# Rewriting the hand-written order of the first stage of a hybrid encoder layer

## The chip, the cores and the metric

The kernel runs on one core of one Trainium2 chip. The metric is the device time of one execution in microseconds; the time of a kernel is the median of its runs. The time before is 1359.33 us (three runs, 1357.09 to 1360.18). One further execution was recorded by the hardware profiler; all views below are of that one.

## The reference

One layer over 4096 tokens of width 1024. An input projection, a windowed attention and a pooling group side by side, gates on both, and an output projection:

```python
h = rmsnorm(x, pre_norm_g)
q, k, v, g_a, u_p, g_p = split(h @ w_in)      # 512,128,128,512,512,512 columns
a = banded_attention(q, k, v, rel_bias, attn_sink) * silu(g_a)   # |i-j| <= 128, 8 heads of 64
p = multiscale_pool(u_p, pool_w, pool_scale) * silu(g_p)         # windows 2, 4, 8, 16, minus the token
mixed = concat([a, p]) @ w_out
out = x + rmsnorm(mixed, post_norm_g)
```

## The kernel before

**Numbers.** Every float32 operand of a large product is split into a float16 high part and a float16 low part; a product is the sum of three float16 products (high by high, low by high, high by low). Weights are scaled by a power of two that comes from their column norms (`sc`, its inverse `isc`), tokens by the inverse root of their row norms.

**Two stages.** The first stage (all of it inside one list, `plan`) computes g_p, g_a and u_p for all tokens and keeps them in DRAM (`ga_scr`, `yp_scr`). The second stage (a second list) computes q, k, v, the attention and the output projection, and is not rewritten by this change except for one operand of `gate`.

**Macro tiles.** The first stage takes 512 tokens at a time: macro tile 0 to macro tile 7. Macro tile 0 is plain: twelve weight tiles of 128 columns (0-3 g_p, 4-7 g_a, 8-11 u_p), four blocks each for tiles 0 and 2 (`mm_block`), one call of `mm` for each of the others. During it the weights are prepared: loaded to one of six `raw` slots, multiplied by the norm gain (`w_fold`, L343), squared (`w_square`, L370), summed over rows (`w_presum` on GpSimd L376, `w_norm` on TensorE L389), turned into the scale (`scale_pow`, five small VectorE steps), split (`w_high` L425, `w_low` L428); the u_p weights are multiplied by `pool_w` first (`u_prod` L355, `u_fold` L363). From pairs of tiles the sums of a Winograd form are built (`t_sums` L444, `t_high` L463, `t_low` L468). Macro tiles 1 to 7 use this form: seven products (`STEPS`) for each of three column groups QU (u_p), QP (g_p), QG (g_a), each product 24 matmuls (`product`, L902).

**Around a product.** After it comes `keep` (ScalarE, L914: the accumulator is copied out), `join` (VectorE, L928: it is added to a kept part) or a direct use (`direct_u`, `direct_gates`). A product that writes the same accumulator next waits for that. Gates are a Sigmoid on ScalarE (L939, L955) and a multiplication (`gate_mult`: GpSimd for QP, VectorE for QG, L946; `direct_mult`, L962). The pooling of the macro tile before (`pool_tile` on VectorE, L775 to L791; `pool_gate` on GpSimd, L799; `pool_store`) stands behind the joins of QU.

**The x of a macro tile.** Four natural blocks are loaded (`x_nat`, L251), squared with an accumulator on ScalarE (L191); the row norms are finished on GpSimd (`x_scale`, L200 and L203), written to DRAM (`rs_row`, L257) and read back spread over all partitions (`rb`, L259). Transposed x is loaded to `ybig` (`y_load`, L269), multiplied by `rb` (`y_scale`, L279), split into `xt` by a ScalarE copy and a VectorE subtraction (`x_hi` L285, `x_lo` L290), and summed in place (`x_sum`, L297).

**Order.** `due(t, fn, ...)` gives every step a planned time; the list is sorted by it, and each engine runs its steps strictly in that order. The planned times decide only the order: an engine whose next step is not ready waits, and all behind it wait with it. All DMAs of the kernel are issued by one queue, SP, in the same order.

Of the kernel before, what the change touches and what calls it, by code (L numbers as in the profile page):

```python
# [17 lines left out]
P = 128  # L18
S = 4096
D = 1024  # L20
# [42 lines left out]
U_EVAC = 2.0**-14  # L63
GP_EVAC = 2.0**-30
GA_EVAC = 2.0**-44
# [4 lines left out]
def hybrid_layer(ctx: ExitStack, tc, io, out):  # L70
# [18 lines left out]
    nc.vector.memset(ones16, 1.0)  # L89
    mhalf = const.tile([P, 1], F32, name="mhalf")  # L90
# [16 lines left out]
    cgs = const.tile([P, 8], F32, name="cgs")  # L107
# [17 lines left out]
    def scale_pow(dst, n2, floor, top):  # L125

        m2 = comm.tile([P, 1], F32, name="m2", tag="m2")
        nc.vector.tensor_reduce(out=m2, in_=n2, axis=mybir.AxisListType.X, op=ALU.max)
# [21 lines left out]
    with ExitStack() as actx:  # L150
# [8 lines left out]
        pw = pa1.tile([P, 4, P], F32, name="pw")  # L159

# [15 lines left out]
        def first_use():  # L176

            nc.scalar.activation(pa1.tile([P, 1], F32, name="dummya"), mhalf, AF.Sigmoid)
# [77 lines left out]
        def rs_row(m):  # L256
            nc.sync.dma_start(rs_scr[m].rearrange("(b p) -> p b", p=P), rs_t[m][:, 1])  # L257
            rb_t[m] = pa1.tile([P, T], F32, name=f"rb{m}", tag="rb")
            nc.sync.dma_start(  # L259
                rb_t[m], rs_scr[m].rearrange("(o t) -> o t", o=1).to_broadcast([P, T])  # L260
            )
# [80 lines left out]
        def w_fold(si, eng=nc.vector):  # L342
            eng.tensor_tensor(out=raw_k(si), in0=raw_k(si), in1=gb, op=ALU.mult)  # L343
# [4 lines left out]
        def u_prod(j, half):  # L348

            wt = raw_of(("u", j))  # L350
            pp = psa.tile([P, 4, P], F32, name=f"wup{j}_{half}", tag="wup", bufs=2)
# [16 lines left out]
        def w_square(si):  # L368
            sq_t[si] = pa.tile([P, KT, P], BF16, name=f"sq{si}", tag="sq")
            nc.scalar.activation(sq_t[si], raw_k(si), AF.Square)  # L370

        def w_presum(si, ns=(4, 2)):

            sq = sq_t[si]
            for n in ns:
                nc.gpsimd.tensor_tensor(  # L376
                    out=sq[:, :n], in0=sq[:, :n], in1=sq[:, n : 2 * n], op=ALU.add
                )

        def w_norm(si, n, by=None, of=None):  # L380

            sq = sq_t.pop(si)
            key = si if of is None else of
            first = key not in n2_t
            if first:
                n2_t[key] = psa.tile([P, 1 if of is None else 2, P], F32, name=f"n2_{key}", tag="n2")
            o = n2_t[key][:, 0 if first else 1]
            for k in range(n):
                nc.tensor.matmul(  # L389
                    o, ones16 if by is None else by[:, k, :], sq[:, k, :],  # L390
                    start=(k == 0 and first), stop=(k == n - 1), skip_group_check=True,
                )

        def w_scale(si):
            scale_pow(
                sc[:, si : si + 1], n2_t.pop(si).rearrange("p a c -> p (a c)"), 1e-20, W_SCALE
            )

        def pair_scale(s1):

            scale_pow(
                sc[:, s1 : s1 + 3 : 2], n2_t.pop(s1).rearrange("p a c -> p (a c)"), 1e-20, W_SCALE
            )
# [7 lines left out]
        def pair_gate(s1):  # L411
            for t, e in ((cg, 1.0), (cgs, 1.0 / (GA_EVAC if s1 >= A_GA else GP_EVAC))):
                nc.vector.tensor_scalar(
                    out=t[:, s1 : s1 + 3 : 2], in0=isc[:, s1 : s1 + 3 : 2], scalar1=e / H_SCALE,
                    scalar2=None, op0=ALU.mult,
                )

# [93 lines left out]
        def row_prod():  # L511
            row_t["p"] = psa.tile([NH, 512], F32, name="fp", tag="wup", bufs=2)
# [71 lines left out]
        def out_scales():  # L584
# [3 lines left out]
                out=rowsc[:, 0:4], in0=isc[:, A_GA : A_GA + 4],  # L588
# [17 lines left out]
        def out_square(k):  # L606
            w = raw_of(("o", k))
            nc.scalar.activation(w, w, AF.Square, scale=rowsc[:, k : k + 1])

        def out_sum(k):  # L610

            sq = raw_of(("o", k))
            if k == KT - 1:
                sq = out_t["s"] = pa.tile([P, D], BF16, name="wosq", tag="sq")
            nc.gpsimd.tensor_tensor(
                out=sq, in0=raw_of(("o", k)), in1=raw_of(("o", k - 1)), op=ALU.add
            )
            raw_put(("o", k - 1))
            if k == KT - 1:
                raw_put(("o", k))  # L620

        def out_norm():
            out_t["n"] = [psa.tile([P, 512], F32, name=f"no{i}", tag="n2") for i in range(2)]
            for i in range(2):
                nc.tensor.matmul(
                    out_t["n"][i], ones16, out_t["s"][:, i * 512 : (i + 1) * 512],
                    start=True, stop=True,
                )

        def out_sigma():  # L630
            nm = pa.tile([P, 2], F32, name="nmx", tag="nmx")
            for i in range(2):
                nc.vector.tensor_reduce(
                    out=nm[:, i : i + 1], in_=out_t["n"][i], axis=mybir.AxisListType.X, op=ALU.max
                )
            scale_pow(sigma, nm, 1e-36, W_SCALE)
# [7 lines left out]


# [86 lines left out]
        def sigmoid(si):  # L732
            nc.scalar.activation(
                plain_dest(si), acc_t[0, si], AF.Sigmoid, scale=cg[:, si : si + 1]
            )

        def silu(si, scale):

            s = plain_dest(si)
# [1293 lines left out]
```

## Time and profile before

| | |
|---|---|
| median of 3 runs | 1359.33 us |
| profiled execution | 1366.74 us, span 1365.0 us |
| mean granted TensorE clock | 0.949 |
| busy: TensorE, VectorE, ScalarE, GpSimd | 1198.0, 979.2, 706.4, 393.8 us |
| last matmul of the first stage ends | 656.5 us after the span's start |

The page of the profile gives busy time by engine; a timeline lists merged instructions with, in brackets, the idle time of that engine before them and what released it; the waits add these up; the groups by line give count, busy time and the mean of one.

### The profile page before, as it was taken

The numbers are of one execution on the slowest core, as the hardware profiler recorded it, in microseconds if no ns is written. First come the engines' busy times: TensorE is split into PE (matmuls) and PEld (weight loads), VectorE is DVE, ScalarE is ACT, GpSimd is POOL, SyncE is SP. The second block draws the span as 40 slices with busy tenths as digits, with TensorE's granted clock in tenths as the row PEclk, the third lists the DMA queues.
The fourth block names the chain that finished last, engine by engine and source line by source line (L and its number), as shares of the span: only waits on it lengthen the run. The fifth ranks groups of instructions, "written<-read, shape, count | busy, mean of one in ns | idle before, by whom it ended". The sixth has DMA issues, their size and how long they took to land. (4 is left out here: it accounts for less than half of the span.)

```text
span 1365.0 us, 25715 instructions
## 1 busy us (share of the span) xinstructions
PE 1198.0 (88%) x10186; PEld 867.8 (64%) x10186; DVE 979.2 (72%) x1800; ACT 706.4 (52%) x1524; POOL 393.8 (29%) x363
## 2 busy tenths in 40 slices
PE   5776859787795859689789999999999999999998
PEld 4532658677684748578666667666676666766654
DVE  5477857565837768584867787777877778777796
ACT  4263624344343626433266666756667566575663
POOL 1120212112243102011212443334433344333431
PEclk9788989989897979889999999999999999999999
DMA  8132735443455557456479577665776567765594
GB/s 226 63 128 72 248 108 198 136 168 111 142 178 175 192 164 248 145 168 184 153 206 254 128 190 202 170 149 154 185 208 170 146 159 182 200 170 139 146 257 122
DMA packets 304569, 230.09 MB, mean 169 GB/s; under 512 B 213776, under 2 KB 270736, under 8 KB 299456
## 3 DMA queue, kind: packets, MB, share of 16 engines
q1 hardware_dynamic: 304448, 228.45, 58.7%
q8 instruction: 79, 1.29, 0.4%
q14 instruction: 42, 0.34, 0.1%
HBM read 115.14 MB, written 62.44 MB: 130 GB/s over the span
## 5 line engine op out<-in xcount | busy, mean ns | idle before, releaser
L902 PEld LDWEIGHTS <-wa 128*128 128x128 f16 x3528 | 357.0, 101 | 123.5 <-issue 71.2
L902 PE MATMUL ch<-xt,wa 128*128 128x256 f16 x2016 | 224.3, 273 | 7.3 <-ACT cbig L914 5.1
L1305 PEld LDWEIGHTS <-raw 128*128 128x128 f16 x1920 | 186.8, 98 | 39.5 <-issue 9.6
L902 PE MATMUL cl<-xt,wa 128*128 128x256 f16 x1008 | 135.4, 304 | 56.7 <-ACT u L950 32.5
L1374 ACT ACTIVATE p<-p,nm 128x385 f32<-128x385 f32 (+1 forms) x256 | 153.0, 599 | 57.2 <-POOL p L1357 38.0
L1404 DVE SCALAR_TENSOR_TENSOR pn<-p,rd,pn 128x384 f16<-128x384 f32 (+1 forms) x256 | 156.6, 658 | 26.1 <-ACT pn L1396 25.4
L1305 PE MATMUL aq<-xt,raw 128*128 128x256 f16 x1536 | 173.1, 273 | 0.0
L1613 PE MATMUL ms<-wo,ys 128*128 128x512 f16 x720 | 162.7, 379 | 0.0
L1363 DVE CUSTOM_DVE_ANT_0 p<-s,ybig,nsink 128x384 f32<-128x384 f32 (+1 forms) x256 | 155.9, 665 | 1.4 <-PE s L1342 1.1
L1396 ACT ACTIVATE pn<-p,rd 128x384 f16<-128x384 f32 (+1 forms) x256 | 136.3, 597 | 23.5 <-ACT p L1374 21.6
L799 POOL TENSOR_TENSOR yt<-yt,gp 128x512 f32<-128x512 f32 x32 | 50.6, 1583 | 323.1 <-DVE yt L791 243.7
L1613 PEld LDWEIGHTS <-ys 128*128 128x128 f16 x720 | 69.1, 98 | 82.8 <-issue 4.2
L1613 PE MATMUL m<-wo,y 128*128 128x512 f16 x540 | 119.6, 379 | 0.6 <-POOL y L1519 0.4
L279 DVE TENSOR_TENSOR ybig<-ybig,rb 128x1024 f32<-128x1024 f32 x28 | 33.4, 1221 | 88.3 <-DMA rb<-rs_scr 83.9
L1613 PEld LDWEIGHTS <-y 128*128 128x128 f16 x540 | 51.5, 98 | 65.2 <-issue 4.4
L1649 POOL TENSOR_TENSOR mo<-mo,ybig 128x512 f32<-128x512 f32 x39 | 64.8, 1661 | 87.5 <-ACT jkb L1638 86.3
L285 ACT CAST xt<-ybig 128x1024 f16<-128x1024 f32 x56 | 57.9, 1036 | 61.0 <-DVE ybig L279 48.1
L290 DVE TENSOR_TENSOR xt<-ybig,xt 128x1024 f16<-128x1024 f32 x56 | 69.5, 1249 | 14.7 <-ACT xt L285 14.7
L1342 PE MATMUL s<-k_all,q 64*128 64x384 f16 (+2 forms) x912 | 73.8, 298 | 3.0 <-ACT q L1295 1.6
L848 PE MATMUL a<-xt,wa 128*128 128x512 f16 x240 | 59.3, 406 | 18.4 <-ACT wa L425 16.8
L1381 DVE TENSOR_SCALAR den<-den 128x4 f32<-128x4 f32 x64 | 17.4, 272 | 76.5 <-ACT p L1374 76.4
L1484 PE MATMUL o<-pt,vv 128*64 128x256 f16 x1128 | 68.1, 274 | 2.8 <-DMA pt<-pn 2.7
(178 smaller groups left out, 1752.8 us busy)
## 6 DMA issues: line engine op xcount, KB each, us to landing
x_scr<-xt SPq DMA_DIRECT2D x16, 1024.0 KB, 4.9
xt<-x_scr SPq DMA_DIRECT2D x15, 1024.0 KB, 7.3
xn<-in_x SPq DMA_DIRECT2D x28, 512.0 KB, 4.9
ybig<-in_xT SPq DMA_DIRECT2D x28, 512.0 KB, 6.1
xr<-in_x SPq DMA_DIRECT2D x28, 512.0 KB, 4.3
out<-xr SPq DMA_DIRECT2D x28, 512.0 KB, 3.8
yp_scr<-yt SPq DMA_DIRECT2D x32, 256.0 KB, 2.5
raw<-in_w_out SPq DMA_DIRECT2D x16, 512.0 KB, 4.6
```

Of the source, the lines that this page charges most:

```text
L290: eng.tensor_tensor(out=o[:, w, 1], in0=y_view(i), in1=o[:, w, 0], op=ALU.subtract)
L848: nc.tensor.matmul(a3, weight(si, wi, k), xt[:, 0:2, k // HK, xi, k % HK, :], start=(n == 0), stop=(n == 3 * KT - 1),)
L902: nc.tensor.matmul(acc[:, c], wa[:, q, wi, slot * HK + k, c * P : (c + 1) * P], x[:, xi, k, :], start=(fresh and n == 0), stop=(n > 3 * 2 ...
L1305: nc.tensor.matmul(acc, w[:, j, k, :], x[:, k // HK, a, k % HK, :], start=(n == 0), stop=(n == 3 * KT - 1),)
L1342: nc.tensor.matmul(s_ps[:, gg, c0:c1], q_t[u, half][a, qi, jj, tl : tl + P], k_all[a, ki, kc : kc + c1 - c0], start=(n == 0 and c0 == 0), ...
L1363: nc.vector.tensor_tensor_reduce(out=p_t[b, half][:, hh, :nk], in0=s_t[b, half][jj][:, gg, :nk], in1=bias[:, h, lo : lo + nk], scale=negc[ ...
L1374: nc.scalar.activation(p[:, hh, : nk + 1], p[:, hh, : nk + 1], AF.Exp, bias=nm_t[b, half][:, hh : hh + 1], scale=-1.0, accum_out=den_t[b, ...
L1396: nc.scalar.activation(prob_view(b, half)[:, 0, i], p_t[b, half][:, i, :nk], AF.Copy, scale=rd_t[b, half][:, i : i + 1],)
L1404: nc.vector.scalar_tensor_tensor(out=pn4[:, 1, i], in0=p_t[b, half][:, i, :nk], scalar=rd_t[b, half][:, i : i + 1], in1=pn4[:, 0, i], op0= ...
L1484: nc.tensor.matmul(o_ps[a, 2 * half : 2 * half + 2], v[:, vi, kt, a], pt[b, half][:, pi, g, :, i, :], start=(n == 0), stop=(n == last),)
L1613: nc.tensor.matmul(z_t[u, tag], y[:, k, yi, :], wo[o][:, wi, k, :], start=(n == 0 and acc is None), stop=(n == 3 * HK - 1), skip_group_che ...
L1649: eng.tensor_tensor(out=mo, in0=mo, in1=gpost[:, cs], op=ALU.mult)
```

## The change

- The gates use the activation Silu in one step (`silus`, `silu`) in place of Sigmoid and a multiplication; `gate_mult` and `direct_mult` go. Because Silu needs the true value, the constant scales move: `keep` and `direct_u` become plain copies, `join` a plain addition; the scale of u_p goes into `pool_gate`, the attention gate's into the second stage's `gate`.
- `pool_gate` moves from GpSimd to VectorE, directly behind `pool_tile`.
- Weight norms: ScalarE squares with an accumulator over the row (`wsq`), and one float32 matmul with `ones32` adds the partitions; the GpSimd sums and the bfloat16 norm matmuls go (tiles 0 and 2 keep a matmul by the squared gain). The same for `w_out` (`osq`).
- The gain is folded on ScalarE in eight pieces (`w_fold_act`) for g_a tiles 4 and 6 and the six tiles of q, k, v.
- `rs_row` no longer reads back: `rs_spread` does, later. The norms of macro tile m+2 are computed in macro tile m.
- In macro tile 1 the attention gate is computed in the plain form (`plain_ga`: four groups of 48 matmuls), ahead of the fourteen Winograd products of QU and QP; the sums of tiles 4 to 7 are built during macro tile 1.
- All planned times of the first stage are new; the steps of `w_b` and `w_out` have fixed places by macro tile.

```diff
 def rs_row(m):
     nc.sync.dma_start(rs_scr[m]..., rs_t[m][:, 1])
+
+def rs_spread(m):
     rb_t[m] = pa1.tile([P, T], F32, name=f"rb{m}", tag="rb")
     nc.sync.dma_start(rb_t[m], rs_scr[m]...to_broadcast([P, T]))
+def w_fold_act(si):
+    for k in range(KT):
+        nc.scalar.activation(raw_k(si)[:, k], raw_k(si)[:, k], AF.Copy, scale=g_pre[:, k : k + 1])
 def w_square(si):
-    sq_t[si] = pa.tile([P, KT, P], BF16, name=f"sq{si}", tag="sq")
-    nc.scalar.activation(sq_t[si], raw_k(si), AF.Square)
-def w_presum(si, ns=(4, 2)):
-    ...nc.gpsimd.tensor_tensor(out=sq[:, :n], in0=sq[:, :n], in1=sq[:, n : 2 * n], op=ALU.add)
+    nc.scalar.activation(junk, raw_of(si), AF.Square, accum_out=wsq[:, si : si + 1])
+def norm_prod(name, rhs):
+    n2_t[name] = psa.tile([P, KT], F32, name=f"n2_{name}", tag="n2")[:, : rhs.shape[1]]
+    nc.tensor.matmul(n2_t[name], ones32, rhs, start=True, stop=True)
 def pool_gate(m, j):
-    nc.gpsimd.tensor_tensor(out=t, in0=t, in1=g_t[m, n][:, c], op=ALU.mult)
+    nc.vector.scalar_tensor_tensor(out=t, in0=t, scalar=usc[:, j : j + 1], in1=g_t[m, n][:, c], ...)
 def keep(m, q, what):
-    nc.scalar.mul(cbig[:, c_t[m, q, what]], flat(acc_t[m, q, "a"]), EV[q])
+    nc.scalar.copy(cbig[:, c_t[m, q, what]], flat(acc_t[m, q, "a"]))
+def silus(m, q, n, h, src):
     for i in range(2):
         si = 4 * q + 2 * n + i
-        nc.scalar.activation(dest(m, q, n, h)[:, i], c[:, i], AF.Sigmoid, scale=cgs[:, si : si + 1])
-def gate_mult(m, q, part, n, h, eng): ...
+        nc.scalar.activation(dest(m, q, n, h)[:, i], src[:, i], AF.Silu, scale=cg[:, si : si + 1])
...
-x_loads(1, t1 - 50.0)
+x_loads(1, (27.0, 33.0), (28.0, 35.0), (36.0, 42.0), (37.0, 44.0))
+due(t1 - 16.0, rs_spread, 1)
...
+def x_ahead(m, t, spread=44.0):
+    if m < NM:
+        x_loads(m, (t + 3, t + 9.3), (t + 4, t + 10.5), (t + 12, t + 24.7), (t + 13, t + 27.2))
+        due(t + spread, rs_spread, m)
...
+            if m == 1:
+                macro_x(1, t0, op_at, t0 + 15.0, op_at(2) + 0.3, (t0 + 34.0, ...))
+                x_ahead(3, t0 + 10.0, 42.0)
+            else:
+                macro_x(m, t0, op_at, t0 + 6.5, t0 + 17.0, (t0 + 21.0, t0 + 22.2, t0 + 27.0, t0 + 28.2))
+                x_ahead(m + 2, t0)
```

In the last lines the arguments of `macro_x` after `op_at` are the planned times of the first pair of `y_load`, of the cast of S4, and of the four `y_scale`.

More of the change, by code (lines that the diff above doesn't have):

```diff
@@ L62 @@
 QKV_EVAC = 2.0**-13
[L63 to L65 removed]
+UP_EVAC = 2.0**-35
+GA_SCALE = 2.0**-35
 P_SCALE = 2.0**14
@@ new lines, in w_norm_raw @@
+        def w_norm_raw(si, of):
+            first = of not in n2_t
+            if first:
+                n2_t[of] = psa.tile([P, 2, P], F32, name=f"n2_{of}", tag="n2")
+            sq = sq_t.pop(si)
+            for k in range(KT):
+                nc.tensor.matmul(
+                    n2_t[of][:, 0 if first else 1], gg[:, k, :], sq[:, k, :],
+                    start=(k == 0 and first), stop=(k == KT - 1), skip_group_check=True,
+                )
+        def w_square(si):
+            junk = pa.tile([P, D], BF16, name=f"wj{si}", tag="sq")
+            nc.scalar.activation(junk, raw_of(si), AF.Square, accum_out=wsq[:, si : si + 1])
@@ L1265, in hybrid_layer @@
+            for i in range(7):
+                for c, q in enumerate(quads):
+                    t = op_at(i) + c * PT
+                    due(t, product, m, i, q)
+                    after(m, i, q, t + PT + 0.1)
         with tc.manual_schedule(engines={E.PE, E.DVE, E.Activation, E.Pool, E.SP}):
```

587 lines of the change are left out of this document (303 added, 284 removed).

## The prediction

> **What bounds the kernel now.** First the page: which engine is busiest.
>
> ```profile
> PE 1198.0 (88%) x10186; PEld 867.8 (64%) x10186; DVE 979.2 (72%) x1800; ACT 706.4 (52%) x1524; POOL 393.8 (29%) x363
> ```
>
> TensorE is the bound, but 88% is an average over two stages. The change touches the first, so second I read TensorE's timeline from the first Winograd product to the first matmul of the second stage.
>
> ```profile
> 138.93 2.78 PE L902 MATMUL ch<-xt,wa 128*128 128x256 f16 x24 [1.08 <-DVE sga L740]
> ...
> 218.68 8.02 PE L902 MATMUL ch<-xt,wa 128*128 128x256 f16 x72
> ...
> 263.99 4.05 PE L902 MATMUL cl<-xt,wa 128*128 128x256 f16 x24 [3.36 <-ACT u L950]
> 278.05 0.37 PE L389 MATMUL n<-sq,ones 128*128 128x128 bf16 x2 [10.01 <-POOL sq L376]
> ...
> 293.35 8.02 PE L902 MATMUL ch<-xt,wa 128*128 128x256 f16 x72
> ...
> 443.53 5.40 PE L902 MATMUL ch<-xt,wa 128*128 128x256 f16 x48
> ...
> 599.84 8.02 PE L902 MATMUL ch<-xt,wa 128*128 128x256 f16 x72
> ...
> 643.21 13.26 PE L902 MATMUL cl<-xt,wa 128*128 128x256 f16 x120 [1.29 <-DVE gp L962]
> 661.15 4.45 PE L1305 MATMUL kv<-xt,raw 128*128 128x256 f16 x24 [4.68 <-DVE u L928]
> ```
>
> Macro tiles 1, 2, 3 and 7 start at 138.93, 218.68, 293.35 and 599.84, macro tile 5 at 443.53; the last matmul ends at 643.21 + 13.26 = 656.47. So macro tile 1 takes 79.8, macro tile 2 74.7, the two after it 75.1 each, 5 and 6 together 156.3, macro tile 7 56.6. In macro tile 7, where no next x is prepared, 384 matmuls take 643.21 - 1.29 - 599.84 = 42.1, or 0.1096 each; the 504 of a macro tile need 55.2. Six macro tiles thus wait about 20 us each. Macro tile 2 shows where: 3.36 for ScalarE's `direct_u`, then 10.01 for a GpSimd sum of squares, and 24 matmuls after the first wait take 4.05 where 2.78 is usual. Third I ask the other engines in that stretch what those two waited for.
>
> ```profile
> 244.18 0.36 SPq L257 DMA_DIRECT2D rs_scr<-ssq  x1
> 253.08 0.33 SPq L259 DMA_DIRECT2D rb<-rs_scr  x1
> ...
> 258.66 3.70 DVE L279 TENSOR_TENSOR ybig<-ybig,rb 128x1024 f32<-128x1024 f32 x3 [11.95 <-DMA rb<-rs_scr]
> ...
> 263.35 0.59 ACT L950 ACTIVATE u<-ch 128x512 f32<-128x512 f32 x1
> 274.96 1.06 ACT L370 ACTIVATE sq<-raw 128x1024 bf16<-128x1024 f32 x1 [10.05 <-DVE raw L343]
> 276.10 1.90 POOL L376 TENSOR_TENSOR sq<-sq 128x512 bf16<-128x512 bf16 x2 [5.16 <-ACT sq L370]
> ...
> DVE ybig L279 <- DMA rb<-rs_scr: 73.8, 6, 17.9
> ACT jk L191 <- DMA xn<-in_x: 26.0, 12, 5.0
> ```
>
> The row of norms is written at 244.18; SP holds its read until the write has landed, 8.9 later, and the read needs 5.6 more. VectorE stands in its order at `y_scale` for 11.95. Behind it stand the x splits ScalarE's `direct_u` is queued after, the gain fold, and through it the square (10.05), the GpSimd sum and the norm matmul on which TensorE waits. One late DMA makes all the waits of the macro tile. It happens six times, 73.8 in all (first of the two rows from the waits; the second is used below).
>
> **The macro tiles.** `rs_row` of macro tile m+2 now stands at about 30 us in macro tile m, `rs_spread` at 44, `y_scale` at 21 of the next one. The write's 8.9 fits in the 14 between, so SP does not hold there, and the read has over 30 us for its 5.6: this wait goes wholly. The GpSimd sums go too, so no norm matmul hangs on GpSimd, whose queue keeps only the finishing of row norms.
>
> The floor: macro tile 1 has 4 x 48 plain and 14 x 24 Winograd matmuls, 528 x 0.1096 = 57.9 (the plain gate costs one product, 2.6); six others 55.2 each. Together 389.1, against 656.47 - 138.93 = 517.5 before: 128.4 less. What is late next? Durations:
>
> ```profile
> L775 DVE TENSOR_TENSOR ws<-u 128x527 f32<-128x527 f32 x22 | 15.4, 702 | 2.3 <-ACT u L762 2.3
> L928 DVE SCALAR_TENSOR_TENSOR cbig<-cl,cbig 128x512 f32<-128x512 f32 x20 | 13.7, 686 | 21.5 <-PE cl L902 21.5
> L687 DVE TENSOR_TENSOR raw<-raw 128x1024 f16<-128x1024 f32 x12 | 16.0, 1336 | 7.0 <-ACT raw L683 7.0
> L343 DVE TENSOR_TENSOR raw<-raw,g_pre 128x1024 f32<-128x1024 f32 x14 | 16.9, 1216 | 0.6 <-DMA raw<-in_w_a 0.6
> L285 ACT CAST xt<-ybig 128x1024 f16<-128x1024 f32 x48 | 49.6, 1036 | 51.5 <-DVE ybig L279 42.1 <-DVE ybig L297 5.6 <-PE cl L902 3.8
> L914 ACT ACTIVATE cbig<-ch 128x512 f32<-128x512 f32 x54 | 30.6, 588 | 25.6 <-PE ch L902 25.6
> L939 ACT ACTIVATE gp<-cbig,cgs 128x256 f32<-128x256 f32 x32 | 14.5, 499 | 53.7 <-DVE cbig L928 53.7
> L762 ACT COPY u<-u 128x16 f32<-128x16 f32 x11 | 2.2, 203 | 1.0 <-DVE u L928 1.0
> L178 ACT ACT_TABLE_LOAD x1 | 1.3, 1283 | 0.7 <-PEq L2023 0.7
> ```
>
> Macro tiles 2 to 4 each hold two weight tiles of q, k, v. I walk the first in the built order, from the macro tile's start with TensorE unhindered. The second product of QU ends at 10.5 and is joined by 11.2. VectorE's next step reduces the norm, and its matmul stands behind the second product of QP: it comes at about 13.4. Queued behind this added wait: five small scale steps and a reciprocal (1, estimated), a pool tile (three steps of 0.70), a join (0.69), a pool tile (four of 0.70), a low part (1.34), the join of QG (0.69): 22.0. For that join ScalarE waits with the gate (2 x 0.50), two casts of x (2 x 1.04) and then `keep` of QU (0.59): 25.7. TensorE wants that accumulator after nine products, at 23.7. So 2.0 lost; I put 2.5 for macro tiles 2 and 3. Macro tile 4 has the first rows of `w_out` as well: two low parts and two sums (4.1 more) on VectorE ahead of the join that frees QU's accumulator: 5. Macro tiles 5 to 7 lack the weight tile, reach the same `keep` at about 21, and lose 1 each. In macro tile 1 two column groups leave each `keep` 2.6 instead of 5.3: 2. Together 15, bounds 0 and 8 per macro tile (56).
>
> Edits at nothing. VectorE gains four `pool_gate` of 0.69 (row of L928) and loses three `gate_mult` and two `direct_mult` of that width. Silu is not in this trace: between the Sigmoid's 0.50 and twice that; 16 per macro tile make 0 to 8 us on ScalarE, whose work in a macro tile with weight tiles I estimate at 36 of 55 (8 casts, 10 `keep` or `direct_u` and 16 gates by the rows of L285, L914 and L939, 22.2; four squares of x at 1.06; per weight tile a fold of 2.6, below, a square and a cast); I take 0. The float32 norm matmul replaces two to eight; 0. Copies for scaled copies: 0. The second stage's `gate` takes one more operand: 0, its nearest row (L928) being that form already.
>
> The gain fold in eight pieces: no row has 128 columns; between L762 (16 columns, 8 x 0.20 = 1.6) and L939 (256 columns, 8 x 0.50 = 4.0). I take 2.6, nearer the middle, against 1.22 on VectorE (L343). ScalarE has 19 spare, VectorE is the late one in the walk, so the price is 0; without that spare it would be 2 x 2.6 per macro tile. The Trainium skill ("ScalarE: Activation LUTs", section "Rules for kernel authors") speaks against this: multiplications belong on VectorE. The trace agrees on the single step, 1.22 against the 2.6 estimated. By the rule the fold would stay on VectorE, which the walk has late: 1.2 more for each of six weight tiles, the sum 7 worse.
>
> **Before the macro tiles.**
>
> ```profile
> 10.38 1.01 PE L389 MATMUL n<-sq,gg 128*128 128x128 bf16 x8 [10.38 <-ACT sq L370]
> ...
> 16.50 1.06 PE L389 MATMUL n<-sq,gg 128*128 128x128 bf16 x8
> 20.02 6.92 PE L835 MATMUL gp<-xt,wa 128*128 128x128 f16 x96 [2.46 <-ACT wa L425]
> ...
> 34.58 2.00 PE L355 MATMUL wup<-pw,raw 128*128 128x128 f32 x16
> ...
> 51.98 3.75 PE L355 MATMUL wup<-pw,raw 128*128 128x128 f32 x16 [4.10 <-DMA raw<-in_w_uT]
> 55.52 6.12 PE L848 MATMUL a<-xt,wa 128*128 128x512 f16 x24
> ...
> 89.42 5.34 PE L848 MATMUL a<-xt,wa 128*128 128x512 f16 x24
> ...
> 124.48 0.61 PE L848 MATMUL a<-xt,wa 128*128 128x512 f16 x1 [10.46 <-ACT wa L425]
> ```
>
> The second norm now stands directly behind the first: done near 12.5 instead of 17.56, and 2.46 later the scaled weights could be ready, at 15. The transposes of x are not shown to be earlier; between 15 and 20.0 I take 16.5, and the blocks end near 30 instead of 34.6. Then one `u_prod` (2.0) and `mm` of tile 1 at 32, where before four `u_prod`, two of them waiting for loads, held it to 55.52. Ten tiles at 5.34 are 53.4, three more `u_prod` 6. I add 8 of waits: tiles 6 and 7 can be loaded only when pair 1 and pair 8 have left their `raw` slots, and the norm matmul on TensorE waits for both squares (bounds 0 and 14). Macro tile 1 starts at 99.4: 39.5 less.
>
> **Into the second stage.** The 4.68 before `kv` goes, since its join no longer stands behind pooling. But VectorE now has four pool tiles behind the last join (18 steps of 0.70), and the first scores need VectorE after them. Between 0 and 4.7 I take 3.
>
> **Sum.** 128.4 - 15 + 39.5 + 3 = 155.9. From the profiled execution's 1366.74 this gives 1210.8. That execution is 7.4 above the median of the runs, 1359.33, so the forecast is 1203 for the median.
>
> **Rivals.**
> - *A new wait at the same place.* `y_load` of Y12 and Y21 waits on SP for the casts of S4 and S3 that use the slots; behind late joins it could land 10 after VectorE reaches `y_scale`. For: it stands behind two gate stores on SP. Against: VectorE reaches it only late itself. Six times 8 beyond my 15: 1203 + 48 = 1251 (1235 to 1290). Chance 0.15.
> - *The norms are still late.* If squares or SP lag a whole macro tile, the 11.95 stays, six times: 1203 + 72 = 1275. Against: over 30 us of slack. Chance 0.03.
> - *Slower: loads hold ScalarE.* Its squares of x, of `w_out` and the folds each wait for a load in order, and every `keep` stands behind them. In the trace such waits last up to 5.0 (26.0 in twelve), then harmless. The saving is 155.9 / 7 = 22 per macro tile; from 4.5 unhidden waits of 5.0 per macro tile on, the kernel is slower; with six, 7 x 30 = 210, 1413. Against: most loads stand 6 us or more ahead. Chance 0.04.
> - *Silu in another table set.* If Silu and the squares or copies around it did not share one set, each of eight gate groups per macro tile would add two loads of 1.28 (row of L178), 20.5 on ScalarE, 36 + 20.5 = 56.5 of 55.2, and the `keep`s late by some 10 per macro tile: 1273. Against: the built program holds one table load per stage, before and after. Chance 0.01. The Trainium skill ("ScalarE: Activation LUTs", section "What ACT_TABLE_LOAD costs") puts a switch at 2.66, of which this trace shows the 1.28 alone; by that estimate 42.6 per macro tile, 78.6 of 55.2, and the kernel would end near 1203 + 7 x 23 = 1364.
>
> **How the numbers follow.** The forecast has 0.76. Its own range: no waits and an early start give 1203 - 15 - 8 = 1180; bounds of 56 and 14 give 1203 + 41 + 6 = 1250. That takes in the first rival's lower half, so the range is 1180 to 1250. Faster by over 0.2% (about the least a measurement of this kernel tells from no change): the forecast and all rivals but the third, 0.76 + 0.15 + 0.03 + 0.01 = 0.95; slower, the third, 0.04; within 0.2%, what lies between it and the others, 0.01.
>
> **What would show it.** After: no idle time of VectorE with `rb` as releaser; no GpSimd release on TensorE; macro tiles 2 to 7 between 55 and 61 apart; macro tile 1 starting at 95 to 105; tile 1's `mm` near 32; first waits inside a macro tile for `keep` in 2 to 4. Macro tiles over 65, or a macro tile 1 start beyond 115, would make it wrong.

## The result and the profile after

| | before | after |
|---|---|---|
| median of the runs | 1359.76 us (4 runs) | 1216.54 us (4 runs, 1215.70 to 1217.60) |
| ratio | | 0.895, 95% interval 0.8934 to 0.8966 |
| profiled execution | 1366.74 us, span 1365.0 | 1217.6 us, span 1215.8 |
| last matmul of the first stage ends | 656.5 | 505.8 |
| mean granted TensorE clock | 0.949 | 0.988 |

The kernel is 143 us faster. TensorE's busy time fell by 34 (1198.0 before), its idle time by 115 (from 1365.0 - 1198.0 = 167.0 to 1215.8 - 1164.1 = 51.7). The page of the profile after:

```profile
PE 1164.1 (96%) x10180; PEld 852.4 (70%) x10180; DVE 928.6 (76%) x1778; ACT 722.2 (59%) x1609; POOL 272.9 (22%) x281
```

Busy times by stretch, one row for the part before macro tile 1 and one for each macro tile. The columns are the stretch, its length, busy time of the five engines, the granted TensorE clock, the DMA share and rate:

```profile
core 0: us, PE busy (x) PEld busy (x) DVE busy (x) ACT busy (x) POOL busy (x), PEclk, DMA share, GB/s
0.00:99.97 99.97, 79.87 (x530) 45.70 (x531) 66.37 (x115) 62.97 (x100) 5.81 (x14) 0.97 0.63 199
99.97:163.42 63.45, 59.47 (x529) 52.51 (x528) 52.53 (x68) 33.55 (x59) 3.67 (x4) 0.97 0.67 179
163.42:220.19 56.77, 55.46 (x511) 49.58 (x509) 38.58 (x61) 35.81 (x74) 1.97 (x2) 1.00 0.78 218
220.19:281.46 61.27, 57.58 (x512) 50.57 (x510) 46.30 (x70) 39.39 (x79) 2.23 (x2) 0.97 0.79 241
281.46:340.77 59.31, 55.62 (x511) 49.53 (x509) 48.36 (x66) 38.72 (x74) 1.87 (x2) 1.00 0.82 222
340.77:395.79 55.02, 55.02 (x507) 49.28 (x505) 45.31 (x71) 30.46 (x52) 2.31 (x2) 1.00 0.81 230
395.79:450.81 55.02, 55.02 (x507) 49.28 (x505) 44.07 (x52) 26.40 (x44) 0.00 (x0) 1.00 0.55 184
450.81:505.83 55.02, 55.02 (x507) 49.28 (x505) 36.77 (x51) 22.51 (x40) 0.00 (x0) 1.00 0.64 196
```

Macro tiles 2 to 4 take 57 to 61 us where they took 75, and macro tiles 5 to 7 take 55.02 with TensorE never idle. TensorE's timeline after, the rows with a wait in the first stage and the way into the second:

```profile
31.75 5.62 PE L864 MATMUL a<-xt,wa 128*128 128x512 f16 x24
...
71.41 0.59 PE L406 MATMUL n<-wsq,ones 128*128 128x2 f32 x2 [6.64 <-ACT wj L402]
...
156.52 7.07 PE L914 MATMUL cl<-xt,wa 128*128 128x256 f16 x48 [3.98 <-DVE u L939]
...
188.61 8.02 PE L914 MATMUL ch<-xt,wa 128*128 128x256 f16 x72 [1.31 <-ACT cbig L926]
...
224.06 2.78 PE L914 MATMUL ch<-xt,wa 128*128 128x256 f16 x24 [1.09 <-DVE cbig L939]
...
248.08 9.69 PE L914 MATMUL ch<-xt,wa 128*128 128x256 f16 x72 [2.39 <-ACT cbig L926]
...
308.16 8.02 PE L914 MATMUL ch<-xt,wa 128*128 128x256 f16 x72 [2.82 <-ACT cbig L926]
...
522.71 0.40 PE L1396 MATMUL s<-k_all,q 64*128 64x256 f16 x2 [6.18 <-ACT q L1349]
...
524.62 7.47 PE L1359 MATMUL aq<-xt,raw 128*128 128x256 f16 x48
```

In the first stage TensorE no longer waits for GpSimd, nor VectorE for `rb`. The longest waits are in other places than before: the norm of weight tiles 4 and 6 (71.41), a join in macro tile 1 (156.52), `keep` in macro tiles 2 to 4, and the first scores of the second stage (522.71). After a longer wait the next matmuls are slow as well: 48 in 7.07 at 156.52, 72 in 9.69 at 248.08, where 5.40 and 8.02 are usual.

Two rows of the waits after, used below:

```profile
ACT k_all L1349 <- DVE ws L801: 11.6, 1, 11.6
ACT oj L645 <- DMA raw<-in_w_out: 11.5, 3, 5.4
```

### The profile page after: what moved, and what is told of

Its sections match the earlier page's. It is cut to its first block, busy times and chain, and to the rows that moved or that the text cites. A ratio compares the mean times of both kernels' runs of the same rounds, so it can differ in the third digit from the quotient of the medians.

```text
span 1215.8 us, 25547 instructions
## 1 busy us (share of the span) xinstructions
PE 1164.1 (96%) x10180; PEld 852.4 (70%) x10180; DVE 928.6 (76%) x1778; ACT 722.2 (59%) x1609; POOL 272.9 (22%) x281
## 5 line engine op out<-in xcount | busy, mean ns | idle before, releaser
L914 PEld LDWEIGHTS <-wa 128*128 128x128 f16 x3360 | 330.3, 98 | 53.5 <-issue 13.9
L914 PE MATMUL ch<-xt,wa 128*128 128x256 f16 x1920 | 214.8, 274 | 7.8 <-ACT cbig L926 6.5
L914 PE MATMUL cl<-xt,wa 128*128 128x256 f16 x960 | 108.1, 275 | 4.8 <-DVE u L939 4.0
L296 DVE TENSOR_TENSOR xt<-ybig,xt 128x1024 f16<-128x1024 f32 x56 | 66.6, 1221 | 27.7 <-ACT xt L291 27.3
L204 POOL TENSOR_SCALAR ssq<-ssq 128x4 f32<-128x4 f32 (+1 forms) x11 | 6.0, 546 | 353.7 <-ACT jk L195 348.0
L1396 PE MATMUL s<-k_all,q 64*128 64x384 f16 (+2 forms) x912 | 73.7, 298 | 8.1 <-ACT q L1349 6.9
L1396 PEld LDWEIGHTS <-q 64*128 64x128 f16 x912 | 37.1, 95 | 41.6 <-issue 12.6
L1538 PEld LDWEIGHTS <-vv 128*64 128x64 f16 x1128 | 59.2, 110 | 7.9 <-issue 6.5
L948 ACT ACTIVATE gp<-cbig,cg 128x256 f32<-128x256 f32 x42 | 19.0, 500 | 72.4 <-DVE cbig L939 72.4
```

Of the source, the lines that this page charges most:

```text
L296: eng.tensor_tensor(out=o[:, w, 1], in0=y_view(i), in1=o[:, w, 0], op=ALU.subtract)
L914: nc.tensor.matmul(acc[:, c], wa[:, q, wi, slot * HK + k, c * P : (c + 1) * P], x[:, xi, k, :], start=(fresh and n == 0), stop=(n > 3 * 2 ...
L1396: nc.tensor.matmul(s_ps[:, gg, c0:c1], q_t[u, half][a, qi, jj, tl : tl + P], k_all[a, ki, kc : kc + c1 - c0], start=(n == 0 and c0 == 0), ...
L1538: nc.tensor.matmul(o_ps[a, 2 * half : 2 * half + 2], v[:, vi, kt, a], pt[b, half][:, pi, g, :, i, :], start=(n == 0), stop=(n == last),)
```

## The experiments

The runs were made on three chips beside runs of the kernel before, whose median there was 1364.2, 1366.0 and 1364.3 us. The kernel after ran on another, where before had 1359.8. So ratios, and places in a trace, are compared rather than microseconds where the difference is small.

| run | median us | ratio to before, 95% interval |
|---|---|---|
| after | 1216.5 | 0.8950, 0.8934 to 0.8966 |
| 1 before, rows ahead | 1355.6 | 0.9932, 0.9905 to 0.9958 |
| 2 before, rows ahead, write later | 1316.7 | 0.9642, 0.9628 to 0.9657 |
| 3 before, row in 16-byte pieces | 1315.9 | 0.9633, 0.9620 to 0.9647 |
| 4 after, rows late again | 1283.7 | 0.9405, 0.9371 to 0.9439 |
| 5 after, Silu undone | 1261.2 | 0.9242, 0.9215 to 0.9269 |
| 6 after, pool gate on GpSimd | 1217.3 | 0.8921, 0.8897 to 0.8945 |
| 7 after, fold on VectorE | 1219.7 | 0.8931, 0.8910 to 0.8951 |
| 8 after, row in 16-byte pieces | 1211.3 | 0.8865, 0.8851 to 0.8879 |
| 9 after, keep ahead of casts | 1221.9 | 0.8950, 0.8928 to 0.8971 |
| 10 after, last pooling early | 1225.7 | 0.8983, 0.8965 to 0.9002 |
| 11 four edits together | 1214.8 | 0.8894, 0.8877 to 0.8912 |
| 12 the four, and the fold on VectorE | 1213.2 | 0.8887, 0.8872 to 0.8903 |

### 1. Of the kernel before, the rows ahead alone

```diff
-            x_loads(m + 1, t + 1.0)
+            if m + 2 < NM:
+                x_loads(m + 2, t + 1.0)
+            due(t + 8.2, rs_spread, m + 1)
...
```

> The kernel before with one part of the change alone: the row of norms of a macro tile is written one macro tile ahead (x_loads for m + 2 in macro tile m, the read of the row for m + 1 at 8.2 us of macro tile m, the loads of macro tile 2 during the weight tiles). Sums of squares on GpSimd, Sigmoid with a multiplication, and the order of the weight tiles stay as before. Theory (the late row makes most of the waits): the 73.8 us in which VectorE waited for rb go, macro tiles fall from 75 to 57-64, the median to 1260-1290. Rival (the row is one of several equal causes: the GpSimd sums, the gates in three steps and the gain fold on VectorE each hold a macro tile): the wait for rb goes, but macro tiles stay at 68 or more and the median above 1310.

A gain of 0.7%, so the theory in that form fell, though the wait for `rb` went but for its first. The waits of this run:

```profile
DVE ybig L281 <- DMA ybig<-in_xT: 57.5, 11, 14.6
DVE ybig L281 <- DMA rb<-rs_scr: 9.5, 1, 9.5
```

VectorE stands at the same `y_scale` for another transfer. SP's queue and VectorE's timeline in macro tile 2 of this run show why:

```profile
254.15 0.36 SPq L257 DMA_DIRECT2D rs_scr<-ssq  x1
254.55 1.06 SPq L271 DMA_DIRECT2D ybig<-in_xT  x2
```
```profile
269.34 2.57 DVE L281 TENSOR_TENSOR ybig<-ybig,rb 128x1024 f32<-128x1024 f32 x2 [10.38 <-DMA ybig<-in_xT]
```

Nobody waits for the row any more, but its write still stands right ahead of `y_load`, which lands 14.8 later. The write is 2 KB in 512 pieces of 4 bytes. What the DMA engines do just after such a write is seen most plainly in the kernel after, where a 512 KB load of `w_out` is issued 0.4 behind one at 257.36. Packets of that trace as a whole, and of the stretch from 257.4 to 266.4, then those of run 1 itself from 254.5 to 263.5:

```profile
DMA packets 304567, 230.08 MB, mean 189 GB/s; under 512 B 213776, under 2 KB 270736, under 8 KB 299456
```
```profile
DMA packets 583, 0.24 MB, mean 27 GB/s; under 512 B 528, under 2 KB 528, under 8 KB 582
```
```profile
DMA packets 886, 0.37 MB, mean 41 GB/s; under 512 B 532, under 2 KB 885, under 8 KB 886
```

For 9 us the DMA engines move 27 and 41 GB/s with loads waiting in the queue. So the write seems not only to land late, but to hold up the transfers behind it (theory W). The next two runs test that.

### 2. The same, with the write behind the loads

```diff
-            due(t + 19.0, rs_row, m)
+            due(t + (30.0 if m > 2 else 19.0), rs_row, m)
```

> The run with the rows ahead alone, and the write of the row (512 pieces of 4 bytes) moved from 20 to 31 us of the macro tile, behind the two y_loads instead of right ahead of them. Theory W (the write's pieces hold up the transfers behind it for about 9 us; there, y_load at 254.55 stood behind the write at 254.15 and landed 14.8 later, and VectorE waited 10.4 for it): the wait for ybig falls to 3 or less, macro tiles 3 to 7 fall from 72-74 to 60-66, the median from 1355.6 to 1285-1315. Rival (y_load is late through its own queue place, the stores of x and of the gates, or the remaining order): the wait stays above 7 and the median above 1335.

39 us less than run 1, 1.7 outside the range named for W (1285 to 1315) and far from the rival. The wait:

```profile
DVE ybig L281 <- DMA ybig<-in_xT: 6.5, 5, 3.3
```

From 57.5 to 6.5 by the place of one 2 KB write. Macro tiles 2 and 3 are now 64.8 and 65.0 long (they start at 219.40 and 284.24, macro tile 4 at 349.20), where the run before had 72.3 and 73.7; what still holds them is the GpSimd sum of squares, for which TensorE waits 2.5 and 5.2 in macro tile 2 and 2.7 and 5.2 in macro tile 3.

### 3. Of the kernel before, the write in 16-byte pieces

```diff
-            nc.sync.dma_start(rs_scr[m].rearrange("(b p) -> p b", p=P), rs_t[m][:, 1])
+            nc.sync.dma_start(rs_scr[m].rearrange("(p b) -> p b", p=P), rs_t[m][:, 1])
```

> The kernel before with one edit: the row of norms is written as 128 pieces of 16 bytes instead of 512 of 4 (it then stands in another order, so tokens get each other's norms; the output is not the reference's). Theory W (the time of the write goes by its pieces): it lands in 2-4 instead of 8.9, the wait of VectorE falls from 11.95 to 5-7 in each of six macro tiles, 30-45 us less, 1315-1330. Rival (a fixed time of a write to DRAM followed by a read of it): unchanged, 1355-1365.

One edit, nothing reordered: 3.7%, about 50 us, more than W had named. Some 8 of it lie ahead of the macro tiles, which W had not counted: macro tile 1 starts at 131.23 here, at 138.93 before. In macro tile 2 of this run SP issues the read 1.45 after the write, where the kernel before needed 8.9; VectorE waits about half:

```profile
229.04 0.33 SPq L257 DMA_DIRECT2D rs_scr<-ssq  x1
230.49 0.33 SPq L259 DMA_DIRECT2D rb<-rs_scr  x1
```
```profile
237.14 4.63 DVE L279 TENSOR_TENSOR ybig<-ybig,rb 128x1024 f32<-128x1024 f32 x4 [5.56 <-DMA rb<-rs_scr]
```

So the cost is not a fixed time of a write and a read. It depends on how the row is cut into pieces; here the pieces became fewer and larger at once, so the number and the size of pieces are not told apart. This is the root of the wait for `rb` that the prediction read off the trace.

### 4. Of the kernel after, the rows late again

```diff
-                x_loads(m, (t + 3, t + 9.3), (t + 4, t + 10.5), (t + 12, t + 24.7), (t + 13, t + 27.2))
-                due(t + spread, rs_spread, m)
+                x_loads(m, *((t + 1.0 + 4 * i, t + 5.5 + 4 * i) for i in range(4)))
+                due(t + 20.9, rs_spread, m)
...
-                x_ahead(m + 2, t0)
+                x_ahead(m + 1, t0)
```

> The changed kernel with that one part undone for macro tiles 3 to 7: their x is loaded, squared and its row written and read within the macro tile just before, at the times that the kernel before had; everything else as changed. Theory: VectorE waits about 10-12 us for rb at y_scale in each of five macro tiles (2 to 6), and since joins and pool tiles stand behind it, 50-75 us come back: 1266-1290. Rival (the new order has no GpSimd sum and no norm matmul behind that wait, so most of it is hidden): VectorE waits as long, but the median rises by under 15, below 1232.

67 us come back (62 by ratio), as the theory had it:

```profile
DVE ybig L285 <- DMA rb<-rs_scr: 74.9, 5, 17.0
PE ch L914 <- ACT cbig L926: 59.3, 9, 11.5
```

Five waits of 15 on VectorE; TensorE's waits for `keep` come to 59, against 6.5 in after: macro tiles 2 to 6 take 70.6, 71.9, 74.6, 67.9 and 67.9. The rest of the new order hides little of a late row. Run 1 and this one do not disagree: in both, one transfer lands late ahead of `y_scale`, by either way.

### 5. Of the kernel after, Silu undone

```diff
-                    dest(m, q, n, h)[:, i], src[:, i], AF.Silu, scale=cg[:, si : si + 1]
+                    dest(m, q, n, h)[:, i], src[:, i], AF.Sigmoid, scale=cg[:, si : si + 1]
...
+                nc.vector.scalar_tensor_tensor(
+                    out=d, in0=src[:, i], scalar=cg[:, si : si + 1], in1=d, op0=ALU.mult, op1=ALU.mult)
...
```

> The changed kernel with Silu undone: ScalarE writes a Sigmoid into the same place, and VectorE multiplies by the accumulator (or the joined sum) and the row's factor, 128x256 at a time, 16 more VectorE steps in a macro tile. Theory: Silu costs ScalarE nothing over Sigmoid (both 0.50 here), and it spares VectorE 16 x 0.35-0.45 = 5.6-7.2 us per macro tile, on the engine that is late in macro tiles 1 to 4, and frees the accumulators of the direct gates earlier: without it 10-30 us more, 1227-1247. Rival (VectorE is busy 76% and has the room): under 5 us, up to 1222.

45 us more (40 by ratio), above the 10 to 30 named. The step added (a group of this run), and what TensorE waits for:

```profile
L957 DVE SCALAR_TENSOR_TENSOR gp<-cbig,cg,gp 128x256 f32<-128x256 f32 x42 | 18.4, 479 | 4.0 <-ACT gp L950 4.0
```
```profile
PE cl L916 <- DVE gp L957: 28.3, 7, 7.6
```

16 x 0.48 = 7.7 per macro tile on VectorE; TensorE waits once in each of the seven macro tiles for a direct gate whose accumulator VectorE must read a second time. The first scores also come 3.3 later (9.47 of waiting instead of 6.18). Before the change GpSimd did a part of these multiplications, so this is not what Silu gave against before; it is what it gives in the new order.

### 6. Of the kernel after, the pool gate on GpSimd

```diff
-            nc.vector.scalar_tensor_tensor(
-                out=t, in0=t, scalar=usc[:, j : j + 1], in1=g_t[m, n][:, c], op0=ALU.mult, op1=ALU.mult)
+            nc.gpsimd.tensor_tensor(out=t, in0=t, in1=g_t[m, n][:, c], op=ALU.mult)
...
```

> The changed kernel with the multiplication by the gate after pooling back on GpSimd, as before the change (a plain product; the factor per row is left out and a constant stands at the evacuation of u in its place, so the output's scale per row differs). Theory A (VectorE and GpSimd slow each other): VectorE has four steps of 0.75 less per macro tile, but the pooling additions beside a GpSimd product take 1.1 instead of 0.70; the two nearly cancel, the median stays within 1212-1224. Theory B (VectorE's length counts, and what is on GpSimd is free): the waits in macro tiles 1 to 4 shrink and the end of the first stage comes 2-3 us earlier: 1205-1213.

No difference that shows, as Theory A had it, though the additions grew from 0.70 to 0.87 (128x527) and 0.98 (128x525) rather than to 1.1. The additions of pooling, of the kernel after and then of this run:

```profile
L789 DVE TENSOR_TENSOR ws<-u 128x527 f32<-128x527 f32 x28 | 19.7, 702 | 4.2 <-ACT u L776 4.1
```
```profile
L789 DVE TENSOR_TENSOR ws<-u 128x527 f32<-128x527 f32 x28 | 24.2, 866 | 4.4 <-ACT u L776 4.2
```

VectorE gives away 28 x 0.75 = 21 us and gets about half of it back as longer additions (4.5 here, 5.6 in the group of 128x525). So `pool_gate` on VectorE at nothing was right.

### 7. Of the kernel after, the gain fold on VectorE

```diff
-            for k in range(KT):
-                nc.scalar.activation(raw_k(si)[:, k], raw_k(si)[:, k], AF.Copy, scale=g_pre[:, k : k + 1])
+            w_fold(si)
```

> The changed kernel with the gain fold of eight weight tiles (4 and 6, and the six of q, k, v) back on VectorE as one multiplication of 1.22, in place of eight pieces of ScalarE (2.44 in all). The prediction's walk: VectorE is late in macro tiles 2 to 4, so 1.2 comes back in each of six weight tiles, about 7 us more, 1221-1225. The rule of the Trainium skill (multiplication belongs on VectorE), taken as a forecast of time: half the work, so no more than now, at most 1217. Third possibility: it stands in VectorE's order where VectorE waits anyway, within 1 us of 1216.5.

By ratio the same as after; the runs spread from 1214.6 to 1224.2. In the profiled one macro tiles 2 to 4 take 56.8, 60.0 and 58.8 against 56.8, 61.3 and 59.3: the fold costs nothing there. Macro tile 1 takes 69.6 instead of 63.5, because `y_scale` waits 4.9 for a `y_load`. That place varies, and more by chip than by edit: `y_scale` waits there 1.5 in after, 1.8 and 2.0 in runs 4 and 6 (one chip), 4.9 here, and 7.6 and 7.1 in runs 9 and 10 (another chip), none of which changes anything up to there; TensorE's wait behind it goes from 3.8 to 10.3. The likely cause, argued and not shown alone, is that a row is written 2 us after that `y_load` is issued, and its 4-byte pieces catch what has not yet drained; with 16-byte pieces `y_scale` waits there 1.9 on the chip of this run (run 8) and 0.2 on that of runs 9 and 10 (run 11, where `y_scale` itself is slower and so comes later). Run 12 settles the fold without this.

### 8. Of the kernel after, the write in 16-byte pieces

The edit of run 3, with the same loss: tokens get each other's norms.

> The changed kernel with the same edit (128 pieces of 16 bytes). Theory W: the loads behind the write (the weight tile 4 in the weight tiles, rows of w_out in macro tiles 2 and 3) land earlier, ScalarE's waits for them (2.9; 5.4 and 4.2) shrink, and with them TensorE's 6.6 before tile 4 and the waits at the start of macro tile 3: 3-10 us less, 1207-1213. Rival (these loads are late for want of a free slot): unchanged within 1 us, 1215.5-1217.5.

0.9% less. The wait of ScalarE for rows of `w_out` is gone from the list, and TensorE's norm of tiles 4 and 6 comes 3 us earlier:

```profile
68.41 0.58 PE L406 MATMUL n<-wsq,ones 128*128 128x2 f32 x2 [3.62 <-ACT wj L402]
```

So the kernel after still paid for the pieces in two places: ahead of the weight loads, and of `out_load`, for which `out_square` held ScalarE.

### 9. Of the kernel after, keep ahead of the casts

```diff
-                    m, t0, op_at, t0 + 6.5, t0 + 17.0,
+                    m, t0, op_at, t0 + 6.5, t0 + (18.6 if m < 5 else 17.0),
```

> The changed kernel with the casts of S4 and S3 in macro tiles 2 to 4 moved from 17.0 to 18.6 us, behind the keep of QU's third product on ScalarE instead of ahead of it (and the two y_loads that follow them 1.6 later). Theory (the walk of the prediction: ScalarE waits with the gate and two casts ahead of that keep): TensorE's waits for cbig of 1.31, 2.39 and 2.82 in macro tiles 2, 3 and 4 go, 4-7 us less, 1210-1213. Rival (the gate ahead of the casts is late by itself, or the later y_load makes VectorE wait at y_scale): under 2 us less, or more than now, 1215-1219.

By ratio the same as after, so the rival, though above the 1215 to 1219 it named. Macro tiles 2 to 4 together take 177.4, as in after (56.77 + 61.27 + 59.31 = 177.35). The waits for `keep` go in macro tiles 2 and 3 and shrink to 0.67 and 0.74 in 4, and others stand in their place; two of this run:

```profile
232.81 7.06 PE L914 MATMUL ch<-xt,wa 128*128 128x256 f16 x48 [2.81 <-DVE cbig L939]
...
281.82 0.39 PE L406 MATMUL n_out<-osq,ones 128*128 128x8 f32 x2 [2.38 <-ACT oj L645]
```

Moving two casts behind a `keep` moved the lateness to the joins and to `out_square`. The walk had the place right; it was not one step that was late there. The profiled execution, the longest of the four, takes 70.6 in macro tile 1, 7.2 more than after's; that is the place named in run 7.

### 10. Of the kernel after, the last pooling early

```diff
-                    pooling(m, 2 * n, t + (14.0 if n else 9.5))
-                    pooling(m, 2 * n + 1, t + (14.5 if n else 10.0))
+                    pooling(m, 2 * n, t + 3.5)
+                    pooling(m, 2 * n + 1, t + 6.0)
...
-            at_(7, 33.0 + 1.2 * h, bias_head, h)
+            at_(7, 27.0 + 0.9 * h, bias_head, h)
```

> The changed kernel with the pooling of the last macro tile moved ahead: its two wide pool tiles from 14 us behind the join of QU's c22 to 3.5 and 6.0, the two narrow ones from 9.5 and 10.0 behind the join of c21 to 3.5 and 6.0, and the attention bias's steps from 33 to 27 us of macro tile 7, which leaves VectorE free there. Theory (ScalarE's first k of the second stage waits 11.6 for memory that the last pool tiles still use, and TensorE 6.18 for it, after which its next 48 matmuls take 7.5 instead of 5.4): the 6.18 falls to under 1, the 48 matmuls take 5.4, 6-8 us less, 1208-1211. Rival (the wait is passed on to the last joins or to the first softmax steps of VectorE, which the same pool tiles then delay): under 3 us less, 1213-1217.

Not faster: by ratio 0.4% above after, with intervals that just touch, and neither reading's figure. The 6.18 did go, and with it the slow matmuls:

```profile
517.19 5.16 PE L914 MATMUL cl<-xt,wa 128*128 128x256 f16 x24 [4.18 <-DVE cbig L939]
...
533.87 0.28 PE L1396 MATMUL s<-k_all,q 64*128 64x256 f16 x2 [0.75 <-ACT q L1349]
...
535.24 5.41 PE L1359 MATMUL aq<-xt,raw 128*128 128x256 f16 x48
```

But the first of these rows is new: a join of QG, which TensorE needs for its last product, stands behind a moved pool tile, and that tile holds VectorE because the place of its result is still being stored:

```profile
514.98 0.69 DVE L805 SCALAR_TENSOR_TENSOR yt<-ws,u 128x512 f32<-128x512 f32 x1 [5.06 <-DMA yp_scr<-yt]
```

Macro tile 7 takes 62.0 instead of 55.0 (7.0 more); from the first k to the first scores 11.5 instead of 16.9 (5.4 less), and from there to the end 690.2 instead of 693.1 (2.9 less): 1.3 gained. The span is 8.3 longer, so 9.6 come from earlier stretches that this edit does not touch; macro tile 1, with its wait of 10.3, has 5.9 of them, the part before it 1.6.

### 11 and 12. Four edits together, without and with the fold on VectorE

The row in 16-byte pieces, read with a stride so that each token keeps its own norm; the edits of runs 9 and 10; and the widest pool tile of macro tile 1 behind the join of 156.52.

```diff
+            r = rb_t[m].rearrange("p (o q b) -> p o b q", o=1, b=BPM)[:, :, 2 * h : 2 * h + 2]
...
+            eng.tensor_tensor(out=y, in0=y, in1=r.to_broadcast([P, HK, 2, P]), op=ALU.mult)
...
-                        pooling(m - 1, 2 * n + 1, t + 2.9 + 0.7 * n)
+                        pooling(m - 1, 2 * n + 1, t + (6.2 if n and m == 1 else 2.9 + 0.7 * n))
```

> The changed kernel with four edits together: the row of norms written as 128 pieces of 16 bytes in the order that they lie in on chip, and y_scale reading it with a stride so that each token gets its own norm again; the last pooling and the bias steps earlier; casts of S4 and S3 behind the keep in macro tiles 2 to 4; and in macro tile 1 the widest pool tile behind the join that TensorE waits for (its 3.98 and the slow matmuls after it). From 1216.5: 5 by the write, 7 by the pooling, 4-6 by the casts, 4-6 in macro tile 1: 1192-1197. Rival: the strided read makes y_scale longer (1.23 now, 28 of them) and takes back what the write gave; twice as long would be 4 x 1.2 per macro tile on VectorE, of which half might show: 1200-1212.

> The same four edits and the gain fold of eight weight tiles on VectorE (one multiplication of 1.22) instead of in eight pieces on ScalarE. The prediction's price: 7 more than the run without it. The earlier run of the fold on VectorE alone had macro tiles 2 to 4 of 56.8, 60.0 and 58.8 against 56.8, 61.3 and 59.3, so by that the difference is -2 to +1; its macro tile 1 was 6 longer behind a late y_load, which the shorter write should take away.

1214.8 and 1213.2 against the 1192 to 1197 hoped for: both are 0.6 to 0.7% below after by ratio, less than the pieces alone gave (run 8). The rival of run 11 is likely one reason. `y_scale` in after and in run 11:

```profile
L285 DVE TENSOR_TENSOR ybig<-ybig,rb 128x1024 f32<-128x1024 f32 x28 | 33.3, 1221 | 6.3 <-DMA ybig<-in_xT 6.3
```
```profile
L286 DVE TENSOR_TENSOR ybig<-ybig,rb 128x1024 f32<-128x1024 f32 x27 | 53.8, 2042 | 0.5 <-DMA ybig<-in_xT 0.5
```

20 us more on VectorE for 6 of waiting taken away. Another is run 10's join: macro tile 7 takes 62.7 and 62.0. The first scores come at 522.34, no earlier than in after (522.71). What each edit gives beside the others was not measured alone. Run 12 has the lowest ratio here with the reference's arithmetic, and its fold on VectorE costs nothing that shows against run 11 (0.8887 and 0.8894, overlapping intervals). Untried is run 12 with the pool tiles behind the join of QG.

## Why the prediction was right

The forecast was 1203, the result 1216.5. Its own sum, against the profiled executions, was 155.9; they differ by 1366.74 - 1217.6 = 149.1.

| step | forecast | measured |
|---|---|---|
| macro tile 1 starts | 99.4 | 99.97 |
| macro tiles 1 to 7 together | 389.1 + 15 = 404.1 | 505.83 - 99.97 = 405.9 |
| into the second stage | 3 less | 1.1 less |
| second stage from the first scores on | unchanged | 2.5 more |

- **The macro tiles.** The floor holds: 55.02 for each tile without a wait, against the 55.2 worked out. The seven macro tiles come to 1.8 more than floor and 15 of waits, but the loss is in other places: macro tiles 1 and 3 are 3.5 and 3.6 longer than forecast, 2 and 4 are 0.9 shorter each, and 5 to 7, put down for 1 each, lose nothing. That the sum came so near is partly luck. The first wait in 2 is for `keep` where the walk had it, 1.31 instead of 2.0, and in 3 and 4 `keep` takes 2.39 and 2.82. In macro tile 1 the walk looked at the `keep`s, which don't wait; the wait is a join behind two pool tiles, 3.98 and then slow matmuls.
- **Why they had been long.** "One late DMA makes all the waits of the macro tile" is about half right. In run 2 VectorE waits only 6.5 in all for `ybig` and once, 8.9, for `rb`, yet macro tiles 2 and 3 take 64.8 and 65.0: some 10 of the 20 us above the floor are left, mostly in the waits for the GpSimd sum. The sum of the forecast did not need the "all", since the change removes the late row and the GpSimd sums both. Putting the row back late costs 67 (62 by ratio, run 4) of the 517.5 - 405.9 = 111.6 that the macro tiles gained; how the rest divides among the GpSimd sums, the gates and the order was not measured. (The 73.8 are the waits for `rb` up to 540 us; in the whole execution there are seven, 83.9.) The prediction also took the write's 8.9 for its own delay, covered by 14 us of slack. Runs 1 to 3 show that it holds back what is queued behind it. In the order of before, with the rows ahead and the write left in front of `y_load`, the gain was 9 (run 1). The first rival, a `y_load` that comes late, thus stood for something real, by another cause than it named (casts and stores ahead of it): VectorE waits 57.5 for it in run 1, and it is the likely cause in macro tile 1 of runs 7, 9 and 10. In macro tiles 2 to 6 of the new order `rs_row` stands at 30, behind the loads at 6.5 and 20.5. The prediction gives no such reason for that place, so for the prediction this part is luck.
- **Before the macro tiles.** Tile 1's `mm` starts at 31.75, forecast 32; no run undoes this part alone. The 8 of waits for tiles 4 to 7 are 6.64 in one; behind it stands not only the slot but, for about 3 us, another row of 4-byte pieces (run 8).
- **Into the second stage.** The wait of `kv` (4.68) went, and the four pool tiles behind the last join did what was feared: ScalarE waits 11.6 for them and TensorE 6.18. The term was mis-sized, 1.1 instead of 3. Before the change the first scores came 18.0 after the end of the first stage, here 16.9; a row of the kernel before:

```profile
674.45 0.28 PE L1342 MATMUL s<-k_all,q 64*128 64x256 f16 x2 [0.94 <-ACT q L1295]
```

- **What no step had.** From the first scores on, the second stage takes 693.1, and 1365.0 - 674.45 = 690.6 before. After the 6.18, 48 matmuls take 7.47 instead of 5.40; runs 10, 11 and 12, without that wait, take 690.2, 690.7 and 689.6.
- **The base.** The forecast for the median took 7.4 off because the profiled execution of before was that much above its median. That of after is 1.1 above its own. So 6.3 of the 13.5 between 1203 and 1216.5 are no step of the change; 1.8 are the macro tiles, 0.6 the start, 1.9 the transition, 2.5 the second stage (the 0.4 left is rounding: 1210.8 - 7.4 is 1203.4).
- **Edits at nothing.** The gate on VectorE: right (run 6). Silu takes 0.50, as Sigmoid; one table load stands in the first stage. The prediction set VectorE's lost multiplications against the four `pool_gate` it gained and put both at nothing; run 5 shows that in this order they would cost 45 (40 by ratio); TensorE waits 28.3 of it for accumulators that VectorE still has to read. The fold: eight pieces take 2.44, forecast 2.6, and cost nothing; but that keeping it on VectorE would be 7 worse was wrong (run 12). The walk charged VectorE's length; the likely reason why that does not show, argued and not tested, is that VectorE has idle time ahead of the next join. Keeping to the rule that was weighed against the change ("ScalarE: Activation LUTs", section "Rules for kernel authors", of the Trainium skill: multiplications belong on VectorE) thus does no harm here; run 12 against run 11 cannot show a gain either.
- **The slower rival** exists in small: `out_square` holds ScalarE for 11.5 in three waits, and macro tile 3 starts with waits of 1.09 and 0.21 that are gone where `out_square` does not wait (run 8).

What was named to show it came: no `rb` on VectorE, no GpSimd on TensorE in the first stage, macro tiles 2 and 4 to 7 from 55.0 to 59.3 and macro tile 3 just above the 61 with 61.3, macro tile 1 at 99.97, tile 1's `mm` at 31.75. The first waits inside a macro tile are for `keep` in 2 and 4; in 3 a join comes first (224.06).

## What to carry to other kernels

Where a wait ends with a DMA, look at what was queued ahead of that DMA, and count its pieces: a 2 KB write in 4-byte pieces cost the kernel before about 50 us, and writing and reading it a macro tile earlier, still ahead of a load, gave 9. An order written by hand passes lateness on: a step moved out of the way of one wait (runs 9 and 10) made another of the same size, so follow the moved step's own waits (its buffer's last store, the join behind it) before counting the gain. Compare macro tile by macro tile in the trace where a difference is under 1%, since one transfer that came late in some runs and not in others (macro tile 1) was as large as the effects tested.

## What the runs showed of the hardware that was not expected

- A write of 512 pieces of 4 bytes takes 8.9 until a read of it can be issued; 128 pieces of 16 bytes, the same 2 KB, take 1.45. In the 9 us behind the first kind the DMA engines moved 27 GB/s with a 512 KB load waiting. The Trainium skill ("DMA: Bandwidth & Descriptors", section "Rules for kernel authors") says that a last dimension which is not contiguous becomes one descriptor per element; the 528 packets under 512 bytes agree. What that does to the transfers behind it is shown here.
- TensorE is slow for a while after some waits: 72 matmuls in 9.69 after 2.39, 24 in 5.16 after 4.18, 48 in 7.47 after 6.18, where 8.02, 2.78 and 5.40 are usual; but 8.02 after 2.82 (308.16), and 9.69 after 2.83 at the same place in run 8. The granted clock is 0.97 in macro tiles 1 and 3, which have such a stretch, and 1.00 in 2, 4 and 5 to 7. The Trainium skill ("TensorE: Matmul & The Clock Gate", section "What's actually happening") gives half the clock after an idle window of about 3.4 us that runs freely. That waits of the same length do and do not cost agrees with a window that runs freely. The wait of 2.39 is shorter than the page's window and yet was followed by slow matmuls; there the measurement differs from the page, and it decides.
- A VectorE product whose second operand is read every 16 bytes took 2.04 instead of 1.22 (run 11; its operands also have one dimension more there, so the stride alone is not shown). Pooling additions in a run with GpSimd products beside them took 0.87 on average instead of 0.70.
